# Hybrid encoder layer: operation costs of the order planner, spacing of the recurrent branch, and PSUM banks of its gates

## The chip, the cores and the metric

The kernel runs on one core of one Trainium2 chip. The metric is the device time of one execution in microseconds (us); less is better. Three executions of the kernel before took 1450.05, 1450.06 and 1452.24 us, median 1450.06. The profiled execution took 1451.69 us, and its trace spans 1449.9 us.

PE is TensorE (matmul; PEld is its weight load), DVE is VectorE, ACT is ScalarE, and SP issues all DMAs.

## The reference, cut to what matters

One layer over 1024 tokens of width 1024, float32, without batch:

```
h = rms_norm(x)
q, k, v, u, y, g_att, g_rec = split(h @ w_in + b_in)        # 512,512,512,1024,1024,1024,1024 columns
y_att = neighbourhood_attention(q, k, v, rpb) @ w_att_o     # 8 heads x 64
u = depthwise_conv4(u, conv_w, conv_b)
h_fwd, h_bwd = rg_lru(u, forward), rg_lru(u, backward)
   # r, i = sigmoid(block_diag(u) + b);  log_a = -8 r softplus(-lam);  a = exp(log_a)
   # h[t] = a[t] * h[t-1] + sqrt(1 - a[t]^2) * i[t] * u[t]
y_rec = ((h_fwd + h_bwd) * gelu(y)) @ w_rec_o
x = x + (sigmoid(g_att) * y_att + sigmoid(g_rec) * y_rec) @ w_out
x = x + square(relu(rms_norm(x) @ w_ff1)) @ w_ff2
return rms_norm(x)
```

## The kernel before, in words

**Number format and products.** Every float32 operand of a large product is split into a high part (an ACT copy with rounding: `wh`, `sh`, `uh`, `rh`) and a low part (a DVE subtraction: `wl`, `sl`, `ul`, `rl`); each product takes three matmuls (high x high, high x low, low x high). Nearly every matmul has a 128x128 weight tile and a 128x512 operand. The input projection and the feed-forward use a seven-product scheme for 2x2 block matrices: sums of weight blocks (`ws`, on DVE) and of activation blocks are formed once, and seven products replace eight.

**Stages, in order of time.** (1) RMSNorm of x, transposes on PE, the product for v, up to about 72 us. (2) The input projection of u, y, g (both gates) and q, k in 20 "pairs" (`pairs`, lines 627 to 654). A pair is seven products of 12 matmuls, 84 in all, on weights that ACT and DVE must have split before; the running sums of a pair (`r0`, `r1`) leave PSUM by an ACT copy or a DVE addition after each product (`ev1` to `ev7`). (3) Beside stage 2 run eight recurrent chains (lines 862 to 975), one per 128 channels of u: ACT adds the bias and takes the first tap of the convolution, DVE the other three (`uc`), a split gives `uh` and `ul`; four gates, each of six matmuls into two PSUM banks (`gate_pe`, lines 894 to 904), each bank evicted by an ACT sigmoid (`gate_act`); then tanh, exp, square, sqrt on ACT, multiplications and two scans on DVE (forward, backward), their sum, and the product with gelu(y). (4) Attention in 64 tiles between the matmuls of the recurrent output projection (`tprod`, lines 836 to 855, evicted by `evyr`, line 1151). (5) Attention output projection (evicted by `evya`, line 1177), output projection with the second norm, and feed-forward.

**What sets the order.** The program is not issued as it is written. A recorder (`Plan`, lines 109 to 332) notes each operation with its operands, a position and a cost in ns (lines 172 to 195). Positions count the steps of the PE main line, one step being six matmuls; `SD(position, ...)` places side work, lower positions first. `solve` (lines 204 to 324) runs a list schedule over these costs: an engine that is free takes the ready operation of lowest position, a pool tile is given when one is free. The operations are then issued in the order of their planned starts, so the costs and positions decide the order in every engine's queue, and nothing else of them reaches the chip. Because the recorder issues all, every instruction has line 332 in the profile.

**Pools.** SBUF tiles: 45 of `t`, 9 of `w`, 48 small ones. PSUM has eight banks of 128x512 float32. Pool `pm` has 2 slots of 128x1024 (two banks each), pool `pa` 4 slots of one bank. The pair products use both (`prod`, line 586); a 128x512 tile of `pm` takes a slot of two banks. Gates, transposes and attention take `pa`; `tprod` takes a whole `pm` slot of 128x1024.

**Placing of the chains.** `PORD` (line 825) is the order of the 20 pairs. A chain of u's pair starts at the end of that pair, the second chain of the pair `RSTEP` = 28 positions later; within a chain a step planned at t us sits t / `RRATE` positions behind the start, `RRATE` = 1.6. The attention tiles start `AOFF` = 3 positions after the products and stand `ASTEP` = 0.8 positions apart.

Tile names: `pa`, `pm` PSUM; `hTh`, `hTl` the transposed norm's two parts; `T1h` to `T4l` sums of these; `wh`, `wl`, `sh`, `sl`, `wx` weight blocks and their sums; `g` gate tiles, `th`, `sq` their temporaries; `r` running sums.

Of the kernel before, what the change touches and what calls it, by code (L numbers as in the profile page):

```python
# [106 lines left out]
class Plan:  # L107
# [11 lines left out]
    def add(self, eng, meth, args, kw):  # L119
# [9 lines left out]
        for v in rd + wr:  # L129
            if v.base.tag in ("pm", "pa"):  # L130
                for o in v.base.acc:
                    if o.eng != eng:
                        op.preds[o.idx] = 1
                v.base.acc.append(op)
# [37 lines left out]
        n = wr[0].free() if wr else 0  # L172
        psum = any(v.base.tag in ("pm", "pa") for v in rd)
        aps = sum(1 for k in ("scale", "bias") if isinstance(kw.get(k), VA))
# [3 lines left out]
        elif eng == "act":  # L178
            op.cost = n / 1.2 + (50 if psum else 94) + (93 if aps else 0) + (93 if "accum_out" in kw else 0)
            fn = args[2].name if hasattr(args[2], "name") else str(args[2]).split(".")[-1]  # L180
# [5 lines left out]
        elif eng == "dve":  # L186
            two = meth in ("tensor_copy", "tensor_scalar") and not psum
            aps = sum(1 for a in args[2:] if isinstance(a, VA) and a.free() == 1)
            op.cost = n / (1.92 if two else 0.96) + 68 + 60 * min(aps, 2) if n > 4 else 90
            if meth == "reciprocal":  # L190
                op.cost = 60 + 6.3 * n
        elif eng == "pool":
            op.cost = n * 2.2 + 60
        else:
            op.cost = 480
# [148 lines left out]
def emit(tc, x, prm, wst, wv, wg, watt, wrec, wout, wff1, wff2, tb, bv, lnf, out):  # L344
    nc = tc.nc
    from contextlib import ExitStack

    plan = Plan({"t": NSLOT - NW, "w": NW, "s": 48, "pm": 2, "pa": 4, "c": 64, "d": 128})
    pe, act, dve, pool, sp = [plan.engine(e) for e in ("pe", "act", "dve", "pool", "sp")]

    with ExitStack() as ctx:
# [18 lines left out]
        def PM():  # L370
            return VT(nm("pm"), (P, 1024), F32, "pm")

# [208 lines left out]
        def prod(o, a, ob, b, key, bank, first, ev, boost=5.0):  # L581

            for kk in range(2):
                def run(kk=kk):
                    if kk == 0 and first:
                        o.ps[key] = VT(nm("pm"), (P, 512), F32, "pm") if bank else PA()
                    hi, lo = o.lhs[a]()
# [168 lines left out]
        for t in range(8):  # L756

            def vq(t=t, o=Obj()):
                def run(q):
                    if q == 0:  # L760
                        o.ps = PM()
                    ps = o.ps[:, :512]
                    w = wvj[q]
# [44 lines left out]
        def st_qk(m):  # L808
            def store(r, half):
# [14 lines left out]

        PORD = (("u", 0), ("y", 0), ("g", 0), ("u", 1), ("y", 1), ("g", 1), ("g", 2), ("u", 2), ("y", 2), ("g", 3),
                ("g", 4), ("u", 3), ("y", 3), ("g", 5), ("g", 6), ("g", 7), ("qk", 0), ("qk", 1), ("qk", 2), ("qk", 3))
        FIRST = {"u": 8, "y": 16, "g": 24}
        STORE = {"u": st_u, "y": st_y, "g": st_g, "qk": st_qk}
        RSTEP, RRATE, AOFF, ASTEP = 28.0, 1.6, 3.0, 0.8
        B0 = here()  # L830
# [5 lines left out]
        def tprod(w, objs, kk=KD, wsel=None):  # L836

            o = Obj()
            for k in range(kk):
                def run(k=k):  # L840
                    if k == 0:
                        o.ps = PM()
                    wh = w.hi if wsel is None else w.hi[:, wsel]
                    wl = w.lo if wsel is None else w.lo[:, wsel]
                    for b in range(2):
                        c = slice(b * 512, (b + 1) * 512)
                        pe.matmul(o.ps[:, c], wh[:, k, :], objs.at("h", k, b * 512, 512), start=(k == 0), stop=False)
                    for b in range(2):
                        c = slice(b * 512, (b + 1) * 512)
                        pe.matmul(o.ps[:, c], wh[:, k, :], objs.at("l", k, b * 512, 512), start=False, stop=False)  # L850
                    for b in range(2):
                        c = slice(b * 512, (b + 1) * 512)
                        pe.matmul(o.ps[:, c], wl[:, k, :], objs.at("h", k, b * 512, 512), start=False, stop=(k == kk - 1))
                o.last = M(run)
            return o
# [6 lines left out]
        for j in range(8):  # L862
# [31 lines left out]
            def gate_pe(ty, d, R=R, j=j):  # L894
                w = wgj[j // 2]
                wh = w.hi[:, j % 2, ty * 2 + d, :]
                wl = w.lo[:, j % 2, ty * 2 + d, :]
                pss = R.g[ty, d] = [PA(), PA()]
                for b in range(2):
# [245 lines left out]
        for j in range(8):  # L1145
# [5 lines left out]
            def evyr(o=o, j=j):  # L1151
                dve.scalar_tensor_tensor(yr[j], yr[j], 1.0, o.ps, ALU.add, ALU.mult)
                yrd[j] = Dr("yrd")
                sp.dma_start(yrd[j], yr[j])
# [14 lines left out]
        for j in range(8):  # L1169
# [7 lines left out]
            def evya(o=o, j=j):  # L1177
                dve.scalar_tensor_tensor(ya[j], ya[j], 1.0, o.ps, ALU.add, ALU.mult)
                dve.tensor_add(ya[j], yr[j], ya[j])
                for b in range(2):  # L1180
                    split(mx.at("h", j, b * 512, 512), mx.at("l", j, b * 512, 512), ya[j][:, b * 512:(b + 1) * 512])
            SD(o.last + 0.1, evya, 30.0)
# [337 lines left out]
        for tag, n in plan.slots.items():  # L1520
            if tag == "c":
                pools[tag] = ctx.enter_context(tc.tile_pool(name="cp", bufs=1))
            elif tag == "d":
                pools[tag] = ctx.enter_context(tc.tile_pool(name="dp", bufs=1, space=bass.MemoryType.DRAM))
            elif tag in ("pm", "pa"):
                pools[tag] = ctx.enter_context(tc.tile_pool(name=tag, bufs=1, space=bass.MemoryType.PSUM))
# [81 lines left out]
```

## Time and profile before

| | before |
|---|---|
| median of three executions | 1450.06 us |
| profiled execution | 1451.69 us |
| span of its trace | 1449.9 us |
| granted TensorE clock, mean over the span | 0.995 |
| PE busy | 1413.8 us, 98% |
| DVE busy | 1043.6 us, 72% |
| ACT busy | 851.2 us, 59% |
| pair products with recurrent chains | 74.79 to 517.70 us, 442.91 us |

A busy share is the time in which an engine had an instruction under way. PE's matmuls overlap, so a busy PE may still start its matmuls further apart than it could; the distance of starts shows that. A wait in the profile is the idle time in front of an instruction, with the instruction that released it. A granted clock of 1.00 is TensorE at its full 2.4 GHz, and a slice's clock below 1.00 means that part of the slice ran at 1.2 GHz.

### The profile page before, as it was taken

How to read it: one execution, taken by the hardware profiler on the slowest of the kernel's cores; microseconds unless marked ns; L12 is line 12 of the kernel's file. 1: busy time of each engine (PE TensorE's matmuls, PEld its weight loads, DVE VectorE, ACT ScalarE, POOL GpSimd, SP SyncE). 2: the span in 40 equal slices, each digit the busy share in tenths (PEclk: the TensorE clock that was granted, in tenths of full speed). 3: DMA queues.
4: the chain of work that ended last, by engine and by line, in shares of the span. 5: the costliest groups of instructions: out<-in, count | busy, mean ns of one | idle time of the engine just before them, and what ended most of it. 6: DMA issues, size and time to landing. Idle time of an engine off the chain costs nothing.

```text
span 1449.9 us, 17675 instructions
## 1 busy us (share of the span) xinstructions
PE 1413.8 (98%) x6544; PEld 1150.9 (79%) x6544; DVE 1043.6 (72%) x1566; ACT 851.2 (59%) x1321; POOL 0.7 (0%) x6
## 2 busy tenths in 40 slices
PE   7999989999999999999999999999999999999997
PEld 5877767777877877787888878888888888888886
DVE  7996777778776477774764687665555867858995
ACT  7857877767864476764535555555555634332543
POOL 0000000000000000000000000000000000000000
PEclk9999999999999999999999999999999999999999
DMA  6514143143233494563923325444447893245402
GB/s 218 155 59 131 54 148 118 59 145 116 102 117 131 156 379 172 197 211 120 412 83 131 112 99 200 163 160 160 148 146 261 291 341 120 95 148 201 139 33 91
DMA packets 86935, 229.04 MB, mean 158 GB/s; under 512 B 8512, under 2 KB 16832, under 8 KB 86848
## 3 DMA queue, kind: packets, MB, share of 16 engines
q1 hardware_dynamic: 86848, 227.91, 45.2%
q8 instruction: 51, 0.84, 0.2%
q14 instruction: 36, 0.29, 0.1%
HBM read 158.67 MB, written 69.21 MB: 157 GB/s over the span
## 4 chain that ended last, share of the span: by engine, by line
PE 54%; DVE 4%; ACT 1%; issue 1%; DVEq 0%; ACTq 0%
PE pa L332 37%; PE pm L332 17%; DVE acc L332 1%; DVE wl L332 1%; DVE rl L332 1%; ACT fo L332 0%; DVE nu L332 0%; DVE h L332 0%; DVE x L332 0%; ACT h L332 0%; DVE F L332 0%; DVE fo L332 0%; DVE nr L332 0%; DVE T2l L332 0%; ACT wh L332 0%
## 5 line engine op out<-in xcount | busy, mean ns | idle before, releaser
L332 PE MATMUL pa<-wh,rh 128*128 128x512 f32 x448 | 174.1, 389 | 0.3 <-ACT rh L332 0.3
L332 PE MATMUL pa<-wl,rh 128*128 128x512 f32 x448 | 174.1, 389 | 0.0
L332 PE MATMUL pa<-wh,rl 128*128 128x512 f32 x448 | 174.0, 389 | 0.0
L332 ACT ACTIVATE r<-r 128x1024 f32<-128x1024 f32 x64 | 67.8, 1060 | 76.6 <-DVE r L332 75.2
L332 ACT ACTIVATE r<-pm 128x512 f32<-128x512 f32 x102 | 59.9, 588 | 73.9 <-PE pm L332 73.9
L332 DVE TENSOR_TENSOR wl<-ws,wh 128x1024 fp32r<-128x1024 f32 x64 | 77.7, 1220 | 33.9 <-ACT wh L332 33.3
L332 ACT ACTIVATE rh<-rs 128x1024 fp32r<-128x1024 f32 x56 | 58.7, 1049 | 70.8 <-PE pa L332 44.1
L332 ACT ACTIVATE sh<-ws 128x1024 fp32r<-128x1024 f32 x72 | 75.9, 1059 | 39.3 <-DVE ws L332 39.1
L332 PEld LDWEIGHTS pa<-wh,rh 128*128 128x128 f32 x448 | 84.0, 188 | 18.0 <-ACT rh L332 0.7
L332 PEld LDWEIGHTS pa<-wl,rh 128*128 128x128 f32 x448 | 84.0, 188 | 17.9 <-DVE wl L332 0.4
L332 PEld LDWEIGHTS pa<-wh,rl 128*128 128x128 f32 x448 | 84.1, 188 | 17.7 <-DVE rl L332 0.2
L332 ACT ACTIVATE wh<-w 128x1024 fp32r<-128x1024 f32 x56 | 58.8, 1051 | 56.7 <-PE pa L332 41.3
L332 PE MATMUL pm<-T4h,wx 128*128 128x512 f32 x272 | 90.0, 391 | 1.7 <-DVE r L332 1.6
L332 DVE TENSOR_TENSOR sl<-ws,sh 128x1024 fp32r<-128x1024 f32 x72 | 87.2, 1217 | 2.7 <-ACT sh L332 2.7
L332 DVE TENSOR_TENSOR r<-pa,r 128x512 f32<-128x512 f32 x74 | 50.7, 685 | 48.1 <-PE pa L332 48.0
L332 DVE TENSOR_TENSOR acc<-pa,acc 128x512 f32<-128x512 f32 x72 | 49.3, 686 | 47.9 <-PE pa L332 47.9
L332 DVE TENSOR_TENSOR wl<-w,wh 128x1024 fp32r<-128x1024 f32 x56 | 68.1, 1217 | 9.5 <-ACT wh L332 8.0
L332 DVE TENSOR_TENSOR rl<-rs,rh 128x1024 fp32r<-128x1024 f32 x56 | 68.2, 1217 | 4.5 <-ACT rh L332 3.0
L332 ACT ACTIVATE wh<-ws 128x1024 fp32r<-128x1024 f32 x61 | 63.7, 1053 | 12.3 <-DMA ws<-in_wff_dram 4.4
L332 PEld LDWEIGHTS pm<-T4h,wx 128*128 128x128 f32 x272 | 51.0, 188 | 13.6 <-DVE r L332 3.0
L332 PE MATMUL pa<-T1h,sl 128*128 128x512 f32 x144 | 56.6, 393 | 0.7 <-DVE sl L332 0.7
L332 PE MATMUL pa<-T1h,sh 128*128 128x512 f32 x144 | 56.7, 394 | 0.0
(229 smaller groups left out, 3665.1 us busy)
## 6 DMA issues: line engine op xcount, KB each, us to landing
rs<-rd SPq DMA_DIRECT2D x56, 512.0 KB, 7.5
ws<-in_wst_dram SPq DMA_DIRECT2D x41, 512.0 KB, 4.2
ws<-in_wff_dram SPq DMA_DIRECT2D x36, 512.0 KB, 4.4
w<-in_wff_dram SPq DMA_DIRECT2D x32, 512.0 KB, 7.8
B<-in_tb_dram SPq DMA_DIRECT2D x32, 384.0 KB, 5.2
x<-in_x_dram SPq DMA_DIRECT2D x16, 512.0 KB, 8.6
gd<-r SPq DMA_DIRECT2D x16, 512.0 KB, 3.0
g<-gd SPq DMA_DIRECT2D x16, 512.0 KB, 7.9
```

What stands on the lines that cost most here:

```text
L332: getattr(eng[op.eng], op.meth)(*[r(a) for a in op.args], **{k: r(a) for k, a in op.kw.items()})
```

## The change

Five edits, of which the first changes no instruction and sets only the planner's input:

1. The costs: an ACT operation of n elements is planned at 0.863 n + 168 ns (before: n / 1.2 + 94, or + 50 from PSUM), a DVE operation at 1.043 n + 151 ns (before: n / 0.96 + 68), a scan at 2.08 n + 151 ns (before: as any other DVE operation); small operations at 160 ns instead of 90.
2. PSUM: `pm` has 2 slots of one bank, a new pool `pr` 2 slots of one bank, `pa` its 4. The gates take `pr` instead of `pa`. `tprod` takes one tile of `pm` and one of `pr`.
3. `evyr` and `evya` work on two halves of 128x512 instead of one 128x1024.
4. `PORD` places u's second to fourth pairs one, one and two places later and y's second and third one earlier each.
5. `RSTEP` 28 to 33, `RRATE` 1.6 to 1.0, `AOFF` 3 to 1, `ASTEP` 0.8 to 0.75.

PE, ACT and SP execute as many instructions of the program as before (6354, 1227 and 534), DVE 24 more (1592 for 1568), all of edit 3.

```diff
         elif eng == "act":
-            op.cost = n / 1.2 + (50 if psum else 94) + (93 if aps else 0) + (93 if "accum_out" in kw else 0)
+            op.cost = n * 0.863 + 168 + (85 if aps else 0) + (190 if "accum_out" in kw else 0)
...
-            op.cost = n / (1.92 if two else 0.96) + 68 + 60 * min(aps, 2) if n > 4 else 90
+            op.cost = n * (0.522 if two else 1.043) + 151 + 60 * min(aps, 2) if n > 4 else 160 + 55 * min(aps, 2)
+            if meth == "tensor_tensor_scan":
+                op.cost = n * 2.08 + 151
+            if "accum_out" in kw:
+                op.cost += 85
             if meth == "reciprocal":
-                op.cost = 60 + 6.3 * n
+                op.cost = 152 + 6.3 * n
...
-    plan = Plan({"t": NSLOT - NW, "w": NW, "s": 48, "pm": 2, "pa": 4, "c": 64, "d": 128})
+    plan = Plan({"t": NSLOT - NW, "w": NW, "s": 48, "pm": 2, "pr": 2, "pa": 4, "c": 64, "d": 128})
...
         def PM():
-            return VT(nm("pm"), (P, 1024), F32, "pm")
+            return VT(nm("pm"), (P, 512), F32, "pm")
+
+        def PR():
+            return VT(nm("pr"), (P, 512), F32, "pr")
...
-        PORD = (("u", 0), ("y", 0), ("g", 0), ("u", 1), ("y", 1), ("g", 1), ("g", 2), ("u", 2), ("y", 2), ("g", 3),
-                ("g", 4), ("u", 3), ("y", 3), ("g", 5), ("g", 6), ("g", 7), ("qk", 0), ("qk", 1), ("qk", 2), ("qk", 3))
+        PORD = (("u", 0), ("y", 0), ("g", 0), ("y", 1), ("u", 1), ("g", 1), ("g", 2), ("y", 2), ("u", 2), ("g", 3),
+                ("g", 4), ("y", 3), ("g", 5), ("u", 3), ("g", 6), ("g", 7), ("qk", 0), ("qk", 1), ("qk", 2), ("qk", 3))
...
-        RSTEP, RRATE, AOFF, ASTEP = 28.0, 1.6, 3.0, 0.8
+        RSTEP, RRATE, AOFF, ASTEP = 33.0, 1.0, 1.0, 0.75
...
                     if k == 0:
-                        o.ps = PM()
+                        o.ps = [PM(), PR()]
...
-                pss = R.g[ty, d] = [PA(), PA()]
+                pss = R.g[ty, d] = [PR(), PR()]
...
             def evyr(o=o, j=j):
-                dve.scalar_tensor_tensor(yr[j], yr[j], 1.0, o.ps, ALU.add, ALU.mult)
+                for b in range(2):
+                    t = yr[j][:, b * 512:(b + 1) * 512]
+                    dve.scalar_tensor_tensor(t, t, 1.0, o.ps[b], ALU.add, ALU.mult)
...
             def evya(o=o, j=j):
-                dve.scalar_tensor_tensor(ya[j], ya[j], 1.0, o.ps, ALU.add, ALU.mult)
-                dve.tensor_add(ya[j], yr[j], ya[j])
                 for b in range(2):
-                    split(mx.at("h", j, b * 512, 512), mx.at("l", j, b * 512, 512), ya[j][:, b * 512:(b + 1) * 512])
+                    c = slice(b * 512, (b + 1) * 512)
+                    t = ya[j][:, c]
+                    dve.scalar_tensor_tensor(t, t, 1.0, o.ps[b], ALU.add, ALU.mult)
+                    dve.tensor_add(t, yr[j][:, c], t)
+                    split(mx.at("h", j, b * 512, 512), mx.at("l", j, b * 512, 512), t)
```

Three places show how it moves instructions. The first is on PE, the third gate of the second recurrent chain, before: six matmuls on `uh` and `ul`, written to tiles 1537 and 1539 of `pa`, between matmuls of the pair (on `T4` in `pm`).

```order
L332 MATMUL pm_1264<-T4l_890,wx_1332 128x512
L332 MATMUL pm_1264<-T4h_811,wx_1332 128x512 x2
L332 MATMUL pm_1264<-T4l_890,wx_1332 128x512
L332 MATMUL pm_1264<-T4h_811,wx_1332 128x512
L332 MATMUL pa_1537<-uh_1209,wh_1030 128x512
L332 MATMUL pa_1539<-uh_1209,wh_1030 128x512
L332 MATMUL pa_1537<-ul_1221,wh_1030 128x512
L332 MATMUL pa_1539<-ul_1221,wh_1030 128x512
L332 MATMUL pa_1537<-uh_1209,wl_1042 128x512
L332 MATMUL pa_1539<-uh_1209,wl_1042 128x512
```

After, the same gate writes tiles 1615 and 1620 of `pr`, and its neighbours are a `T1` product in `pa` and a `T3` product in `pm`.

```order
L336 MATMUL pa_1596<-T1l_997,sh_1498 128x512
L336 MATMUL pa_1596<-T1h_666,sl_1510 128x512
L336 MATMUL pr_1615<-uh_1298,wh_986 128x512
L336 MATMUL pr_1620<-uh_1298,wh_986 128x512
L336 MATMUL pr_1615<-ul_1533,wh_986 128x512
L336 MATMUL pr_1620<-ul_1533,wh_986 128x512
L336 MATMUL pr_1615<-uh_1298,wl_1040 128x512
L336 MATMUL pr_1620<-uh_1298,wl_1040 128x512
L336 MATMUL pm_1506<-T3h_627,sh_1498 128x512
L336 MATMUL pm_1506<-T3l_871,sh_1498 128x512
```

The gate no longer shares a pool with the products, and it stands at the boundary of two products instead of inside one. Over stage 2, the gates of the eight chains lie further apart: the last of them stood 443 matmuls before the stage's end, and stands 211 before it now.

The second place is on DVE, at the end of the second chain, before: the scans stand as SCALAR_TENSOR_TENSOR on three `g` tiles, and `wl_1800` is the low part of a weight block that PE waits for.

```order
L332 TENSOR_TENSOR g_1568<-g_1568,th_1606 128x1024
L332 SCALAR_TENSOR_TENSOR g_1522<-g_1481,g_1522 128x1024
L332 TENSOR_TENSOR sl_1774<-ws_1535,sh_1761 128x1024
L332 SCALAR_TENSOR_TENSOR g_1568<-g_1548,g_1568 128x1024
L332 TENSOR_TENSOR g_1780<-g_1780,uc_1556 128x1024
L332 TENSOR_TENSOR wl_1800<-ws_1754,wh_1789 128x1024
L332 TENSOR_TENSOR g_1522<-g_1522,g_1568 128x1024
L332 TENSOR_TENSOR sl_1813<-ws_1589,sh_1802 128x1024
L332 TENSOR_TENSOR g_1522<-g_1522,y_1731 128x1024
```

After, the same end of the second chain:

```order
L336 TENSOR_TENSOR sl_1840<-ws_1690,sh_1824 128x1024
L336 TENSOR_TENSOR g_1598<-g_1598,th_1679 128x1024
L336 SCALAR_TENSOR_TENSOR g_1598<-g_1560,g_1598 128x1024
L336 TENSOR_TENSOR g_1668<-g_1668,th_1687 128x1024
L336 TENSOR_TENSOR sl_1890<-ws_1715,sh_1878 128x1024
L336 SCALAR_TENSOR_TENSOR g_1668<-g_1633,g_1668 128x1024
L336 TENSOR_TENSOR wl_1915<-ws_1837,wh_1887 128x1024
L336 TENSOR_TENSOR r_318_1913<-pa_1880,r_318_1913 128x512
L336 TENSOR_TENSOR g_1895<-g_1895,uc_1734 128x1024
L336 TENSOR_TENSOR g_1598<-g_1598,g_1668 128x1024
```

The second scan still stands ahead of a weight's low part, but the two summed weights `sl` and the multiplications around it are dealt out differently, and the rest of the chain (the sum of both directions) comes two places later.

The third place is on ACT in the first stage, where `h` is the square sum of a tile of x, `ns` a root, `wh` a high part of v's weights and `hTh` the eviction of transposes that v's product reads, before:

```order
L332 ACTIVATE wh_210<-ws_100 128x1024
L332 ACTIVATE h_220,ss_221<-x_105 128x1024
L332 ACTIVATE ns_227<-ss_221,epst_79 128x1
L332 ACTIVATE h_238,ss_239<-x_118 128x1024
L332 ACTIVATE hTh_156<-pa_249,pr_88 128x128 x2
L332 ACTIVATE hTh_165<-pa_249,pr_88 128x128 x2
```

After:

```order
L336 ACTIVATE h_213,ss_214<-x_108 128x1024
L336 ACTIVATE ns_222<-ss_214,epst_82 128x1
L336 ACTIVATE h_227,ss_228<-x_121 128x1024
L336 ACTIVATE ns_236<-ss_228,epst_82 128x1
L336 ACTIVATE h_239,ss_240<-x_127 128x1024
L336 ACTIVATE ns_254<-ss_240,epst_82 128x1
L336 ACTIVATE h_258,ss_259<-x_195 128x1024
L336 ACTIVATE hTh_157<-pa_261,pr_91 128x128 x2
L336 ACTIVATE hTh_166<-pa_261,pr_91 128x128 x2
```

Two more square sums (of `x_127` and `x_195`) and two more roots stand ahead of the second group of `hTh`.

## Rows read from the trace of the kernel before

**Rows 1.** The page's busy times; share of the span, instructions.
```profile
PE 1413.8 (98%) x6544; PEld 1150.9 (79%) x6544; DVE 1043.6 (72%) x1566; ACT 851.2 (59%) x1321; POOL 0.7 (0%) x6
```

**Rows 2.** Windows: us; PE, PEld, DVE, ACT, POOL busy (instructions); clock, DMA share, GB/s.
```profile
74.79:517.70 442.91, 426.84 (x1826) 342.24 (x1824) 329.51 (x367) 308.29 (x367) 0.00 (x0) 0.99 0.34 118
181.25:217.50 36.25, 32.61 (x128) 25.12 (x127) 28.41 (x26) 28.79 (x33) 0.00 (x0) 0.91 0.42 148
290.00:326.25 36.25, 34.09 (x143) 27.49 (x142) 28.14 (x29) 22.91 (x31) 0.00 (x0) 0.95 0.41 145
498.00:540.00 42.00, 41.82 (x203) 33.69 (x202) 30.25 (x46) 32.90 (x47) 0.00 (x0) 1.00 1.04 370
906.25:942.50 36.25, 36.25 (x162) 30.01 (x161) 22.67 (x30) 19.88 (x24) 0.00 (x0) 1.00 0.49 163
```

**Rows 3.** Chain of waits, one piece: start, length, engine, tile, instructions.
```profile
1137.05 238.05 PE pa L332 x1049
```

**Rows 4.** PE's waits in stage 2: us in total, times, longest.
```profile
PE pa L332 <- DVE r L332: 2.9, 2, 2.2
PE pm L332 <- DVE wl L332: 2.6, 1, 2.6
PE pm L332 <- ACT r L332: 1.8, 3, 1.0
PE pa L332 <- ACT uh L332: 1.6, 2, 0.9
PE pm L332 <- DVE r L332: 1.6, 2, 1.4
PE pm L332 <- ACT wh L332: 1.5, 2, 1.1
PE pa L332 <- ACT g L332: 1.0, 1, 1.0
PE pa L332 <- DVE ul L332: 0.9, 2, 0.6
PE pm L332 <- DVE sl L332: 0.8, 1, 0.8
PE pa L332 <- DVE sl L332: 0.7, 1, 0.7
PE pm L332 <- ACT sh L332: 0.5, 1, 0.5
```

**Rows 5.** Timeline, a gate before: start, length, work, [idle in front <-releaser].
```profile
149.12 0.67 ACT L332 ACTIVATE g<-pa,pr 128x512 f32<-128x512 f32 x1
...
150.64 1.25 ACT L332 ACTIVATE g<-pa,pr 128x512 f32<-128x512 f32 x2
...
151.36 0.50 PE L332 MATMUL pa<-uh,wh 128*128 128x512 f32 x1 [0.98 <-ACT g L332]
```

**Rows 6.** Timeline, DVE and PE at the end of the second chain.
```profile
183.60 2.28 DVE L332 TENSOR_TENSOR_SCAN g<-g,g 128x1024 f32<-128x1024 f32 x1
...
185.81 1.20 DVE L332 TENSOR_TENSOR sl<-ws,sh 128x1024 fp32r<-128x1024 f32 x1
...
186.92 2.28 DVE L332 TENSOR_TENSOR_SCAN g<-g,g 128x1024 f32<-128x1024 f32 x1
...
189.12 1.20 DVE L332 TENSOR_TENSOR g<-g,uc 128x1024 f32<-128x1024 f32 x1
...
190.24 1.22 DVE L332 TENSOR_TENSOR wl<-ws,wh 128x1024 fp32r<-128x1024 f32 x1
...
191.51 0.79 PE L332 MATMUL pm<-hTh,wl 128*128 128x512 f32 x1 [2.63 <-DVE wl L332]
...
192.53 0.63 PE L332 MATMUL pa<-T1h,sh 128*128 128x512 f32 x1
...
192.96 0.63 PE L332 MATMUL pa<-T1l,sh 128*128 128x512 f32 x1
```

**Rows 7.** Timeline, ACT in the first stage.
```profile
19.74 1.14 ACT L332 ACTIVATE hTh<-pa,pr 128x128 fp32r<-128x128 f32 x4 [2.15 <-PE pa L332]
```

More of the change, by code (lines that the diff above doesn't have):

```diff
@@ L129, in add @@
         for v in rd + wr:
-            if v.base.tag in ("pm", "pa"):
+            if v.base.tag in ("pm", "pr", "pa"):
                 for o in v.base.acc:
@@ L172, in add @@
         n = wr[0].free() if wr else 0
-        psum = any(v.base.tag in ("pm", "pa") for v in rd)
+        psum = any(v.base.tag in ("pm", "pr", "pa") for v in rd)
         aps = sum(1 for k in ("scale", "bias") if isinstance(kw.get(k), VA))
@@ L585, in run @@
                     if kk == 0 and first:
-                        o.ps[key] = VT(nm("pm"), (P, 512), F32, "pm") if bank else PA()
+                        o.ps[key] = PM() if bank else PA()
                     hi, lo = o.lhs[a]()
@@ L761, in run @@
                         o.ps = PM()
-                    ps = o.ps[:, :512]
+                    ps = o.ps
                     w = wvj[q]
@@ L841, in run @@
                     if k == 0:
-                        o.ps = PM()
+                        o.ps = [PM(), PR()]
                     wh = w.hi if wsel is None else w.hi[:, wsel]
                     wl = w.lo if wsel is None else w.lo[:, wsel]
[L845 to L853, printed above, removed]
+                    for wt, part in ((wh, "h"), (wh, "l"), (wl, "h")):
+                        for b in range(2):
+                            pe.matmul(o.ps[b], wt[:, k, :], objs.at(part, k, b * 512, 512),
+                                      start=(k == 0 and wt is wh and part == "h"),
+                                      stop=(k == kk - 1 and wt is wl))
                 o.last = M(run)
@@ L1151, in evyr @@
             def evyr(o=o, j=j):
-                dve.scalar_tensor_tensor(yr[j], yr[j], 1.0, o.ps, ALU.add, ALU.mult)
+                for b in range(2):
+                    t = yr[j][:, b * 512:(b + 1) * 512]
+                    dve.scalar_tensor_tensor(t, t, 1.0, o.ps[b], ALU.add, ALU.mult)
                 yrd[j] = Dr("yrd")
@@ L1524, in emit @@
                 pools[tag] = ctx.enter_context(tc.tile_pool(name="dp", bufs=1, space=bass.MemoryType.DRAM))
-            elif tag in ("pm", "pa"):
+            elif tag in ("pm", "pr", "pa"):
                 pools[tag] = ctx.enter_context(tc.tile_pool(name=tag, bufs=1, space=bass.MemoryType.PSUM))
```

## The prediction

> **What bounds the kernel now.** I read the page's busy times first, then the table of windows, then the waits of PE, then the timeline where a wait is long. The page says that TensorE sets the time: PE is busy in 98% of the span, DVE in 72%, ACT in 59% [rows 1]. A faster DVE or ACT is therefore worth only what PE stands idle or runs slowly. How much that is follows from PE's own best rate in this trace. In one piece of the chain of waits 1049 matmuls take 238.05 us, 0.2269 us each [rows 3]. The window at 906 us agrees: 162 matmuls in 36.25 us, PE busy throughout, clock 1.00 [rows 2].
>
> The change aims at the stretch of the 20 pairs with the eight recurrent chains, 74.79 to 517.70 us, 442.91 us long [rows 2]. It holds 20 x 84 products less the 48 that ran before 74.79 us, and 8 x 4 gates of 6: 1632 + 192 = 1824 matmuls. At 0.2269 us they would take 413.9 us. The excess is 29.0 us, and it is the whole of what this stretch can give.
>
> The excess has three parts. (1) Idle: 442.91 - 426.84 = 16.1 us [rows 2], in the table of waits as 18 waits of 15.9 us [rows 4]. (2) A lowered clock: the slices at 181 us and at 290 us show 0.91 and 0.95 [rows 2]. There, behind waits on weights, matmuls start 0.43 us apart (192.53, 192.96) [rows 6] instead of 0.227, that is at 1.2 GHz; I count 18 of them in the stretch, 18 x 0.20 = 3.6 us. (3) The rest, 29.0 - 16.1 - 3.6 = 9.3 us: starts further apart at the foot of each wait (a matmul that starts late counts as busy until its modelled end), and bubbles too short to be a wait.
>
> The waits by what they are for [rows 4]: low and high parts of weight blocks (`wl`, `wh`, `sl`, `sh`) 2.6 + 1.5 + 0.8 + 0.7 + 0.5 = 6.1 us; the bank of a gate (`pa` on DVE's `r` and on ACT's `g`) 2.9 + 1.0 = 3.9; the running sums that keep a `pm` bank 1.8 + 1.6 = 3.4; the gates' own operands (`uh`, `ul`) 1.6 + 0.9 = 2.5.
>
> **The costs.** The planner before takes any DVE operation of 1024 elements for 1024 / 0.96 + 68 = 1135 ns. The timeline shows such operations 1.11 to 1.13 us apart (185.81 to 186.92, 189.12 to 190.24), so that is right, but the scans hold DVE for 2.20 us (183.60 to 185.81, 186.92 to 189.12) [rows 6]. 16 scans x 1.07 us = 17 us of DVE work in this stretch are unplanned. What comes of it stands at 183 to 192 us: `wl` is issued at 190.24, behind two scans, and PE waits 2.63 us for it, then runs at half clock [rows 6]. With 2.08 n + 151 = 2281 ns the planner knows of it. The other costs rise to the whole duration (1219 ns for 1024 elements, against 1.22 us shown), which overstates what an operation keeps its engine by some 8%. That makes the plan cautious; it puts no work on an engine.
>
> Here one rule speaks otherwise. The Trainium skill, page "VectorE: DVE Perf Modes", section "The DRAIN you can't avoid", says that the next DVE operation doesn't start until the pipe is empty. By that rule an operation would hold DVE for its whole 1.22 us, and the new costs would be exact. The trace disagrees here: the operation of 1.20 us at 189.12 is followed 1.12 us later by one that waits for nothing of it [rows 6]; the same section exempts what is not held. I go by the distance of starts. By the rule DVE's heaviest pair would come to 21.9 us instead of 20.2, at most 1 or 2 us more in all.
>
> **The spread of the chains.** I put the order of DVE's and ACT's instructions, cut at each pair's last running sum, beside the distances of starts. A pair gives PE 84 x 0.227 = 19.1 us, with its share of gates 21.3 us. Before, DVE has 24.6 us in one pair and 21.8 to 21.9 in four more, ACT 24.8 and 22.6 in two, while the last eight pairs ask DVE for only 8 to 16. In the windows this shows as DVE busy for 28.4 and ACT for 28.8 of 36.25 us at 181 us [rows 2], near full where a chain crosses the weights. After, DVE has at most 20.2 and ACT over 21.3 once (22.2). So weights and operands are late in at most one or two pairs: of 6.1 + 2.5 us of waits I leave 2.5. The chain's own length, 31.5 positions instead of 20, delays nothing that PE needs soon: the last gate still stands 211 matmuls, 48 us, ahead of the recurrent output projection.
>
> **The banks.** The products keep `pa` to themselves: gates no longer take banks there, which removes 3.9. A product's tile in `pm` was followed by its successor in as few as 11 matmuls, now in 24 at the least; 24 x 0.227 = 5.4 us is ample for an eviction of 0.6 to 0.7 us, and I leave 1 of 3.4. In exchange the gates have two banks where they had four. A gate can start only when the gate before it was evicted by its two sigmoids. By the order, 17 of 31 gates follow at 4 to 6 matmuls, 0.9 to 1.4 us, the others at 8 or more. A sigmoid takes 0.67 us, and PE starts some 0.05 us behind it [rows 5]: 0.72 us if ACT is free, so nothing; if ACT has just begun another operation of 1.1 us, up to 0.98 us of wait, as one gate shows [rows 5]. Bounds: 0 and 17 x 0.98 = 16.7 us. ACT is busy for 308.29 of 442.91 us, 70% [rows 2]; half a blocked operation in 70% of cases is 0.4 us, less the slack of 0.2 on average: 17 x 0.2 = 3.4, and with its tails I take 4.5.
>
> **Start, attention, end.** On ACT the norms of two more x tiles stand ahead of the second group of `hTh`. ACT had idled 2.15 us there for the transposes [rows 7], which covers nearly two square sums of 1.06 us; I take +0.8 (from -0.3 to +1.5). At the stage's end DMA is saturated, share 1.04 [rows 2]; the last of the recurrent loads now stands behind q, k and three gathers of v on SP's queue, with some 3 to 5 us in hand: 0, at worst +4. The 24 added half-width DVE operations lie where DVE has room (22.67 of 36.25 us in the feed-forward is typical [rows 2]): 0. Later stages keep their order: 0.
>
> **Sum.** Of 29.0 us stay: weights and operands 2.5, sums 1.0, gates 4.5, the short bubbles' irreducible part and remaining tails 0.8: 8.8 back, 20.2 gained. With the start, 20.2 - 0.8 = 19.4, and 0.6 for some attention bubbles that denser tiles fill: 20.0. The profiled execution took 1451.69 us, 1.6 above the median: 1451.69 - 20.0 = 1431.7, in the median's terms 1430.1. I say 1430.
>
> **Rivals.** (a) *The gates starve on two banks.* Each gate waits for the sigmoids of the one before. For it: 17 tight successions, an ACT that is 70% busy, and 0.98 us where this happened once [rows 5]. Against it: sigmoids are placed right behind their gates. Price: 31 x 0.98 = 31 us against 25 us that the rest of the excess gives: 1450 - 25 + 31 = 1456. It decides from 25 / 31 = 0.8 us a gate. In this connection the Trainium skill, page "TensorE: Matmul & The Clock Gate", section "A second HAM failure mode: psum-queue depth-cycling", tells of a kernel in which cycling PSUM banks made PE idle briefly and its clock swing. Here the clock fell behind waits of 2 to 3 us on weights [rows 2, 6], and no row shows that short gate waits lower it.
>
> (b) *The waits move.* Costs that overstate make other work late: a weight's part that was early is now issued after a chain's step. Then only banks and sums give, 3.9 + 3.4 us less the new gate waits: 0 to 7, around 1445. For it: the second scan still stands ahead of a `wl` on DVE. Against it: the loads per pair.
>
> (c) *Nothing is gained*, because gates lose what scans give: within 2.9 us of 1450, 0.2%, about what a measurement of this kernel can tell from no change.
>
> **How the numbers follow.** Forecast 0.64 (1421 to 1438; 1421 is 1450 - 29, all the excess); (b) with a gain over 0.2% 0.22 (1438 to 1447); (c) 0.07; (a) or a late recurrent load 0.07. Faster 0.64 + 0.22 = 0.86, same 0.07, slower 0.07. The range leaves out half of (b)'s upper end, (c) and (a): 1420 to 1445.
>
> **What would show it.** Stretch 2 should take about 423 us. PE's waits there on `wl`, `wh`, `uh`, `ul` should shrink from 8.6 to about 2.5 us, waits of `pa` or `pm` banks on `r` from 2.9 + 1.8 + 1.6 = 6.3 to 1, new waits of `pr` on ACT's `g` should come to 2 to 5 us, and no slice should show a clock under 0.98. The forecast is wrong if `pr` waits exceed 10 us, if weights still cost over 5, or if the start or the stage's end takes more than 4 us.

## The result, and the profile after

The changed kernel takes 1440.31 us in the median (four executions, 1439.58 to 1440.83), the kernel before 1450.05 us beside it: ratio 0.9933, interval 0.9916 to 0.995. The gain is 9.7 us, where 20 were forecast. The stage that the change aims at gave more than forecast (26.7 us for 20.2); attention, from which the forecast took 0.6 us of gain, lost 10.4.

The windows of the changed kernel: the whole product stage, the same two slices as in [rows 2], and the attention stage; columns as there.

```profile
78.29:494.51 416.22, 414.54 (x1825) 341.97 (x1824) 333.60 (x379) 308.32 (x366) 0.00 (x0) 1.00 0.36 125
181.25:217.50 36.25, 36.25 (x161) 30.03 (x160) 32.34 (x34) 32.56 (x38) 0.00 (x0) 1.00 0.31 102
290.00:326.25 36.25, 36.25 (x162) 30.01 (x161) 34.32 (x36) 24.20 (x29) 0.00 (x0) 1.00 0.30 103
494.51:679.24 184.73, 184.73 (x1090) 143.20 (x1089) 121.17 (x314) 117.64 (x240) 0.00 (x0) 1.00 0.59 200
```

The product stage takes 416.2 us for 442.9: of the 29.0 us of excess, 26.7 are gone, more than the 20.2 forecast. Both slices now hold 161 and 162 matmuls, as many as the slice at 906 us of [rows 2], where PE never idles. The clock is 1.00 in both. The waits of PE in that stage (columns as in [rows 4]) have shrunk from 15.9 us to 1.7; there is no row for `wl`, `wh`, `sl`, `uh` or `ul`, and none for `pr`:

```profile
PE pm L336 <- ACT r L336: 0.7, 1, 0.7
PE pa L336 <- ACT r L336: 0.7, 1, 0.7
PE pa L336 <- DVE T1l L336: 0.3, 1, 0.3
```

The attention stage of the kernel before, the row to hold against the last window above:

```profile
517.70:692.02 174.32, 173.88 (x1089) 137.58 (x1088) 122.49 (x306) 115.70 (x238) 0.00 (x0) 1.00 0.61 208
```

The same matmuls take 184.7 us instead of 174.3. PE counts as busy throughout in both, so neither a busy share nor the table of waits shows these 10.4 us. They show in the instructions that write or read `V`, 384 records for 192 matmuls (each is two records), first before, then after:

```profile
517.70:692.02 174.32, 34.92 (x384) 24.93 (x384) 1.00 0.61 208
```

```profile
494.51:679.24 184.73, 45.55 (x384) 31.55 (x384) 1.00 0.59 200
```

These are the products of the attention probabilities (`ab`) with v. One head has 64 columns, so its matmul fills half of PE's columns (`128*64` in the rows); the code issues three matmuls for one head and three for the other alternately. The timeline of PE in the kernel before shows a group of all six (x12) and the matmul behind it:

```profile
606.88 0.88 PE L332 MATMUL pa<-ab,V 128*64 128x128 f32 x12
607.69 0.73 PE L332 MATMUL pm<-rh,wh 128*128 128x512 f32 x2
```

Six matmuls take 0.81 us from start to the next start. In the changed kernel:

```profile
593.16 0.87 PE L336 MATMUL pa<-ab,V 128*64 128x128 f32 x6
593.96 0.51 PE L336 MATMUL pm<-rl,wh 128*128 128x512 f32 x1
594.39 0.87 PE L336 MATMUL pa<-ab,V 128*64 128x128 f32 x6
595.19 0.44 PE L336 MATMUL pa<-kh,qs 128*128 128x384 f32 x1
```

(`kh` and `qs` are the operands of the attention scores.) Here each head's three stand alone, and three take 0.80 us, as long as six alternated. Counted in the order of both kernels' instructions, 123 of these matmuls are followed at once by one of the other head before, 64 after; these are called alternations below. The groups, unbroken rows of such matmuls, rise from 41 to 58.

The stretches of all runs, from the starts of the first matmul of each stage in the traces (us; "start" is up to the first product of the pairs on one of the sums `T`, behind 48 others; "FF1" goes from the first matmul on `B11` to the first of the second feed-forward product, which is "FF2"). The stretches are those of one execution of each kernel, the median is that of all: the executions of the kernel before ran from 1447.4 to 1452.6 us, those with the lowest times at a granted clock of 0.999 and those with the highest at 0.995, so a few us of a difference between two stretches can be the execution's.

| | start | products | attention | to FF1 | FF1 | FF2 | median |
|---|---|---|---|---|---|---|---|
| before | 74.8 | 442.9 | 174.3 | 131.5 | 313.4 | 304.9 | 1450.1 |
| after | 78.3 | 416.2 | 184.7 | 130.6 | 317.1 | 304.0 | 1440.3 |
| av_pair | 77.8 | 416.2 | 166.4 | 130.6 | 317.1 | 304.0 | 1421.7 |
| pair_seq | 78.5 | 416.2 | 174.8 | 130.6 | 317.0 | 304.0 | 1430.1 |
| before_av_pair | 74.8 | 442.1 | 168.7 | 131.4 | 313.4 | 304.9 | 1445.2 |
| costs_only | 77.0 | 445.7 | 186.0 | 130.8 | 317.1 | 304.0 | 1471.0 |
| old_costs | 75.3 | 429.0 | 179.5 | 131.5 | 313.4 | 304.9 | 1443.4 |
| banks_only | 75.5 | 438.8 | 174.9 | 131.5 | 313.4 | 304.9 | 1448.8 |
| spread_only | 74.8 | 428.9 | 175.1 | 131.4 | 313.4 | 304.9 | 1438.6 |
| banks_back | 77.6 | 423.6 | 184.7 | 130.6 | 315.5 | 304.0 | 1446.7 |
| scan_true | 75.6 | 419.5 | 179.5 | 131.5 | 313.4 | 304.8 | 1434.1 |
| small_old | 77.2 | 417.7 | 184.7 | 130.6 | 316.2 | 304.0 | 1438.6 |
| mix_pair | 75.2 | 414.4 | 166.9 | 131.5 | 313.4 | 304.8 | 1416.1 |
| mix_pair_att | 74.6 | 414.4 | 168.5 | 131.5 | 313.4 | 304.9 | 1417.5 |
| same_half2 | 75.7 | 414.4 | 178.2 | 131.5 | 313.4 | 304.9 | 1428.0 |
| four_alt2 | 75.3 | 414.4 | 165.8 | 131.6 | 313.4 | 304.9 | 1415.0 |

### The profile page after: what moved, and what is told of

The parts are those of the page before. It is cut to its first block, busy times and chain, and to the rows that moved or that the text cites. A ratio compares the mean times of both kernels' runs of the same rounds, so it can differ in the third digit from the quotient of the medians.

```text
span 1439.0 us, 17698 instructions
## 1 busy us (share of the span) xinstructions
PE 1413.8 (98%) x6544; PEld 1159.2 (81%) x6544; DVE 1042.2 (72%) x1590; ACT 854.2 (59%) x1321; POOL 0.7 (0%) x6
## 4 chain that ended last, share of the span: by engine, by line
PE 97%; DMA 1%; DVE 1%; ACT 1%; issue 0%; SPq 0%
PE pa L336 56%; PE pm L336 33%; PE pr L336 8%; DMA x<-in_x_dram 1%; DMA ws<-in_wv_dram 0%; ACT h L336 0%; DVE T4l L336 0%; DVE T1l L336 0%; ACT hTh L336 0%; DVE h L336 0%; ACT r L336 0%; DVE sl L336 0%; ACT ns L336 0%; DVE nu L336 0%; ACT F L336 0%
## 5 line engine op out<-in xcount | busy, mean ns | idle before, releaser
L336 ACT ACTIVATE r<-r 128x1024 f32<-128x1024 f32 x64 | 67.7, 1060 | 68.2 <-DVE r L336 66.9
L336 ACT ACTIVATE sh<-ws 128x1024 fp32r<-128x1024 f32 x72 | 75.6, 1056 | 31.0 <-DVE ws L336 25.1
L336 DVE CUSTOM_DVE_ANT_0 ab<-pa,B 128x384 f32<-128x384 f32 x64 | 35.4, 556 | 39.6 <-PE pa L336 38.8
L336 ACT ACTIVATE ab<-pa 128x384 f32<-128x384 f32 x64 | 31.0, 484 | 45.6 <-PE pa L336 45.4
```

What stands on the lines that cost most here:

```text
L336: getattr(eng[op.eng], op.meth)(*[r(a) for a in op.args], **{k: r(a) for k, a in op.kw.items()})
```

## The experiments

**The two heads (av_pair, pair_seq, before_av_pair).** The edit gives the planner two more edges, so that the matmuls of both heads are planned when both are ready:

```diff
-            act.activation(o.pt, pt[:, :384], AF.Copy)
+            o.cp = act.activation(o.pt, pt[:, :384], AF.Copy)
...
-                    pe.matmul(ps[o.hd * DH:(o.hd + 1) * DH, o.n * P:(o.n + 1) * P],
+                    mm = pe.matmul(ps[o.hd * DH:(o.hd + 1) * DH, o.n * P:(o.n + 1) * P],
...
+                    mm.preds.setdefault(o0.cp.idx, 1)
+                    mm.preds.setdefault(o1.cp.idx, 1)
```

> The changed kernel with one edit: in attention, the product of the probabilities with v of two heads (12 records of 64 columns) is planned only when both heads are ready, so that their matmuls alternate. Theory (the loss in attention is lost alternation of the two heads): in the changed kernel a matmul followed by the other head's takes 0.122 us, by the same head's 0.233, at a group's end 0.301; alternations rise from 64 to 155 and groups fall from 58 to about 34, so 41.5 us of these matmuls become about 29, with their entries about 14 us less: attention stage 184.7 to about 171 us, time 1440.3 to about 1426. Rival (the stage is longer because its tiles stand denser and engines wait for one another): no change beyond 2 us, 1438 to 1442.

Measured 1421.73 us against 1440.31: 18.6 us less, attention 166.4. The theory holds, and the gain is larger than its 14 us. It had 12.5 from the matmuls themselves and some 1.5 from the entries, the matmuls in front of the groups. By the distances of starts in both traces the matmuls gave 14.4 (41.5 to 27.1) and the entries 5.8 (15.5 to 9.7); other places took some 2 back.

In pair_seq the two loops over heads and blocks are exchanged besides:

```diff
-            for b in range(3):
-                g = b + o0.hf
-                for o in (o0, o1):
+            for o in (o0, o1):
+                for b in range(3):
+                    g = b + o0.hf
```

> As av_pair, but the three matmuls of one head are issued before the three of the other: as few groups as in av_pair, nearly no alternation (29). Theory: alternation itself is what pays: 29 x 0.122 + 129 x 0.23 + 34 x 0.28 = 42.7 us against 41.5 in the changed kernel, some 2 us back at the entries: about 1439.5, attention stage about 184. Rival (what costs is the switch between 128-column and 64-column matmuls, so only the number of groups counts): as fast as av_pair, attention stage 171 to 175 us.

Measured 1430.13 us, attention 174.8: between the two. The theory's 184 us is missed by 9; of the rival, the 171 to 175 us of attention came true, but not that it is as fast as av_pair. Its groups of six:

```profile
580.96 1.14 PE L336 MATMUL pa<-ab,V 128*64 128x128 f32 x12
582.04 0.50 PE L336 MATMUL pm<-rl,wh 128*128 128x512 f32 x1
```

A group takes 1.08 us instead of 0.81, but less than twice the 0.80 of a lone head. By single records, the second head's first matmuls start beside the last ones of the first head: the overlap doesn't need strict alternation, it needs both heads in PE's queue near each other. So of the 18.3 us that av_pair takes from the stage, 9.9 come from having both heads in one group (with it the groups fall from 58 to 35) and 8.4 from alternating them.

> The kernel before with the same one edit as av_pair: alternations rise from 123 to 159. Theory: 36 x 0.11 us, with fewer groups about 4 us less in the attention stage (174.3 to about 170), time 1450 to about 1446. Rival (the stage's length comes from its density): no change.

Measured 1445.15 us against 1451.77 for before beside it (ratio 0.9957, 0.9943 to 0.997), attention 168.7: the same loss was in the kernel before, smaller. The theory's 4 us came out as 5.6 in the stage.

**Why it pays (same_half2, four_alt2).** Both are mix_pair (below) with groups of four tiles, and two banks for the two query groups. The order inside a group of 12 matmuls differs (same_half2 first, four_alt2 with the second line instead):

```diff
+                    for o in (o0, o2) if h == 0 else (o1, o3):   # same head, other query group and bank
...
+                    for o in (o0, o1) if h == 0 else (o2, o3):   # other head, other columns
```

> mix_pair with the matmuls of four attention tiles (two heads, two query groups) planned when all four are ready, 12 matmuls a group, the two query groups in PSUM banks of their own. Order: matmuls of one head alternate between the two query groups, so always the same 64 columns of PE and always another PSUM bank; then the other head. Theory (the two column halves of PE work beside each other): 0.17 to 0.23 us a matmul inside a group, as where heads don't alternate, 192 x about 0.18 = 34 us, time 1421 to 1426. Rival (a matmul that accumulates where the one before it did must wait for it; any other target will do): 0.12 us a matmul, time 1415.

> The same groups of four tiles and the same two banks, but the two heads alternate, as in mix_pair. Theory: 0.12 us a matmul inside a group; 17 to 20 groups instead of 34 take another 2 us from entries and exits unless the longer wait for four tiles makes gaps: time 1414 to 1417. If grouping is worth nothing: 1416 to 1418.

A group of 12 matmuls (x24) and what follows, in same_half2 and then in four_alt2:

```profile
605.82 2.46 PE L345 MATMUL pa<-ab,V 128*64 128x128 f32 x24
608.20 0.45 PE L345 MATMUL pa<-kh,qs 128*128 128x384 f32 x1
```

```profile
600.50 1.53 PE L345 MATMUL pa<-ab,V 128*64 128x128 f32 x24
601.97 0.45 PE L345 MATMUL pa<-kh,qs 128*128 128x384 f32 x1
```

2.38 us against 1.47. Alternating the place of accumulation gains nothing; alternating the column halves does. 1427.99 and 1415.02 us: the theory holds, the rival falls. same_half2 came out 2 us above its range, four_alt2 inside, 1.0 us below mix_pair. The two column halves also write to different halves of PSUM's partitions, and these runs don't tell which of the two lets them overlap.

**The costs (costs_only, old_costs, scan_true, small_old).** costs_only is the kernel before with edit 1 alone, old_costs the changed kernel without it.

> The kernel before with the new costs alone (edit 1): old banks, old order of pairs, old spacing. Theory: the costs bring most of what the product stage gained (of 26.7 us some 15), and they are also what breaks the alternation in attention (62 alternations in its order, as in the changed kernel's 64): stage of products about 428 us, attention about 185, time about 1448. Rival: the banks and the spacing bring the gain, the costs only the loss: products 440 us or more, time 1460.

Measured 1470.98 us, 19 us slower than before (ratio 1.014, 1.0124 to 1.0156). Attention loses as expected (186.0 us); the rest of the theory falls: products 445.7 us, none of the gain. PE's largest waits in the stage are again for gate operands, running sums and weights:

```profile
PE pa L336 <- ACT uh L336: 4.3, 3, 1.9
PE pm L336 <- ACT r L336: 3.8, 6, 0.7
PE pm L336 <- ACT wh L336: 3.3, 4, 1.3
```

The rival (products 440 us or more) is right, though its 1460 us is 11 short: start, attention and FF1 lose 2.2, 11.7 and 3.7 us here.

> The changed kernel with the costs of before (edit 1 undone), banks and spacing new. Theory (banks and spacing bring the gain in the product stage, the costs bring only the losses at the start, in attention and at the second norm): products 418 to 424 us against 416.2 in the changed kernel and 442.9 before, start 75 us as before, attention with 90 alternations in its order about 180 us against 184.7: time about 1433. Rival (the products need the scans' true cost too): products 430 us or more, time 1443 or more.

Measured 1443.39 us, products 429.0. Losses at the start and at FF1 are gone, as the theory has it, but its 418 to 424 us of products are missed, and the rival's 430 only by 1: of the 26.7 us gained, 14.0 come without the costs and 12.7 need them. In attention either edit breaks the alternation alone: the costs with the old placing (costs_only, 62 alternations, 186.0 us), and the new placing with the old costs (old_costs, 90, 179.5). Where both are old it stays at 122 to 124 (banks_only 174.9, spread_only 175.1 us). What PE waits for in the products of old_costs:

```profile
PE pm L332 <- DVE r L332: 5.7, 5, 1.6
PE pr L332 <- DVE ul L332: 1.1, 2, 0.9
PE pr L332 <- ACT g L332: 0.7, 1, 0.7
PE pr L332 <- ACT uh L332: 0.2, 1, 0.2
```

The running sums wait on DVE. Four of the five waits stand at the end of a stretch of DVE without a pause of 0.15 us or more that holds one or two scans; the fifth, of 1.3 us, has no scan in its stretch. scan_true adds to old_costs one line:

```diff
+            if meth == "tensor_tensor_scan":
+                op.cost = n * 2.08 + 151
```

> old_costs (banks and spacing new) with one cost of the new ones: the scan's, 2281 ns instead of 1135. Theory of the prediction (the 17 us of scans that the planner did not know of are what made weights and operands late): products fall from 429.0 to 420 us or less, time from 1443.4 to about 1434. Rival (it is the caution in all other costs, whole durations plus hand-over, that keeps waits away): products 426 to 430 us, time 1441 or more.

Measured 1434.06 us, products 419.5, and the 5.7 us are gone; all that is left in the stage's table:

```profile
PE pr L334 <- ACT g L334: 0.7, 1, 0.7
PE pr L334 <- ACT uh L334: 0.2, 1, 0.2
```

The theory holds. The scan's cost, put in first, is 9.4 us of the 12.7 that the costs give here; all other costs together are 3.3.

> The changed kernel with the cost of one-column DVE operations at 90 ns again (now 160). Theory (the chain of one-column operations between a norm's square sum and its scaling, planned too long, is put behind other work and makes PE's transposes late): products begin at about 75.5 us instead of 78.3, the stretch from B11's to the second feed-forward product 313.5 instead of 317.1, attention unchanged at 184.7: time about 1434. Rival (the costs of the large operations reorder these places): start and that stretch as in the changed kernel, time 1440.

Its edit is `else 90` for `else 160 + 55 * min(aps, 2)`. Measured 1438.57 us, start 77.2, FF1 316.2. The interval (0.99 to 0.9928, against 0.9916 to 0.995) doesn't separate it from the changed kernel; the waits do. The first line is the changed kernel's wait for the scaled tile `h` of the first norm's last tile, the second the changed kernel's wait in FF1, the third the same wait here:

```profile
55.55 1.09 PE L336 MATMUL pa<-ident,h 128*128 128x128 f32 x8 [1.26 <-DVE h L336]
825.13 1.96 PE L336 MATMUL pa<-ident,h 128*128 128x128 f32 x8 [3.37 <-DVE h L336]
824.60 1.09 PE L336 MATMUL pa<-ident,h 128*128 128x128 f32 x8 [2.52 <-DVE h L336]
```

All five runs with the new costs throughout (after, av_pair, pair_seq, costs_only, banks_back) have the first wait, 1.26 us each; here it is gone. So the theory holds for this wait and for a part of FF1's (1.0 us in the kernel before); the rest of FF1's comes from the other costs. With all old costs there (old_costs, mix_pair) FF1 takes 313.4 us as before.

**Banks and spacing (banks_only, spread_only, banks_back).** banks_only is the kernel before with edits 2 and 3; spread_only has the new `PORD` and `33.0, 1.0, 3.0, 0.8`; banks_back is the changed kernel with

```diff
-                pss = R.g[ty, d] = [PR(), PR()]
+                pss = R.g[ty, d] = [PA(), PA()]
```

> The kernel before with the new PSUM pools and the halved evictions alone (edits 2 and 3), costs and spacing old. Theory: only waits for banks go, 3.9 us of gates and about 2 of running sums, so products about 437 us and time about 1444. Rival (pa and pm banks were what upset the whole stage): products 425 us or less, time 1433. Second rival (two banks starve the gates of a chain that runs at the old pace): products above 443 us, slower than before.

> The kernel before with the new order of pairs and the spread chains alone (edit 4 and the first two numbers of edit 5). Theory: the even load takes most of the 8.6 us of waits for weights and gate operands with their clock and restart losses, products about 428 us, time about 1436. Rival (the chains lie closer in time of gates and products, so the shared banks go on costing): products 437 us or more, time 1445.

> The changed kernel with the gates back in the pool of the products (pa, four banks); pr is used by the recurrent projection alone. Theory: gates and products wait for each other's banks again, 4 us of waits and as much of restarts: products 422 to 426 us, time about 1447. Rival (with spread chains the pool does not matter): products within 2 us of 416, time about 1440.

banks_only: products 438.8, 4.1 us less; near its theory's 437, but its time is 1448.84 us, not 1444, near no change (ratio 0.999, 0.9981 to 0.9999). The waits for banks fall, as the theory has it, from 7.3 us (`r` 6.3, `g` 1.0) to 2.9, but those for `sl` rise from 1.5 us to 7.1. This is rival (b) of the prediction, waits that move:

```profile
PE pm L332 <- DVE sl L332: 5.0, 5, 1.6
PE pa L332 <- DVE sl L332: 2.1, 3, 0.8
```

spread_only: products 428.9, time 1438.63, near its theory (428, 1436): the largest single part, and alone as fast as all five edits together (ratio 0.992, 0.9907 to 0.9934, against 0.9916 to 0.995). banks_back: products 423.6, 1446.69, as its theory, though of its 5.9 us of waits 3.2 are for banks (`r`, `g`) and 2.4 for `sh` and `sl`. The second rival of banks_only (two banks starve the gates) falls.

**Costs where they help (mix_pair, mix_pair_att).** mix_pair is av_pair with

```diff
+            if self.lo <= self.pos < self.hi:     # lo, hi: first pair, recurrent projection
...
+            else:                                 # the costs of before
```

> av_pair with the new costs for work of the product stage alone (positions from the first pair to the recurrent projection); before and behind it the planner gets the costs of before. Theory (the new costs gain in the product stage and lose at the start, in attention and at the second norm): start 75.2 us, products 416 to 419, attention about 166.5 with 158 alternations, the stretch from B11's to the second feed-forward product 313.4 instead of 317.1: time about 1417 against 1421.7 for av_pair. Rival (the product stage's gain hangs on the order that the start leaves): products 425 us or more, time 1426.

Measured 1416.06 us (ratio to before 0.9758, 0.9745 to 0.9771), 24.3 us less than the changed kernel. Its two stages:

```profile
75.17:489.59 414.42, 413.96 (x1826) 342.12 (x1824) 329.94 (x368) 307.97 (x366) 0.00 (x0) 1.00 0.36 125
489.59:656.47 166.88, 166.87 (x1090) 132.82 (x1088) 120.78 (x314) 117.45 (x241) 0.00 (x0) 1.00 0.65 225
```

The products are 0.5 us from the 413.9 of PE's own rate, below the 416 to 419 expected. The theory holds.

> mix_pair with the attention tiles placed as before (AOFF 3.0, ASTEP 0.8). Theory (with alternation held, the placing of the tiles matters little): attention 166 to 169 us, time within 3 us of mix_pair. Rival (denser tiles cost by themselves, as old_costs with 179.5 against spread_only with 175.1 us seems to say): 4 us less than mix_pair.

Measured 1417.48 us, attention 168.5: placing matters by 1.6 us once the heads are kept together. The rival falls: the 4.4 us between old_costs and spread_only came with lost alternation (90 against 124).

## Why the prediction missed, step by step

**Attention, 0.6 us gained: this step failed.** It measured 10.4 us lost. The prediction read "denser tiles" from the positions and looked for engines that wait; it took an idle-free PE for one whose time is fixed by its matmuls, and said of costs that overstate an operation that they only make the plan cautious. The runs show that the new costs reorder other stages too: alone they make the kernel 19 us slower (costs_only), 11.7 of it in attention, where the two heads' matmuls alternate 62 times instead of 123. Neither the scan's cost nor that of the small operations does it (attention is the same in scan_true as in old_costs, and in small_old as in the changed kernel), so it comes from the rest of the costs. The order of the instructions is fixed before a run, so a count of the alternations (123 against 64) would have shown this without one. With the alternation repaired (av_pair) the kernel takes 1421.7 us, below the forecast 1430.

That 1440.3 us lies within the range given, 1420 to 1445, is luck: the products gained 6.5 us more than forecast, and attention, start and later stages lost 10.4, 3.5 and 1.9. By its time the result falls where the prediction put rival (b), 1438 to 1447, but in the product stage the waits shrank instead of moving. (The stretches sum to 10.9 us, the medians differ by 9.7: the profiled execution of the kernel before was 1.6 us above its median.) Of the signs that were to show the forecast wrong none came true, and none of them looked at attention.

**Products, 20.2 us gained.** Measured 26.7. The parts: spacing alone 14.0, banks alone 4.1, costs alone -2.8; together 26.7. The sum of single effects is 15.3, so 11.4 lie in their interplay. Under the old costs the banks add nothing to the spacing (spread_only 428.9, old_costs 429.0); under the new costs they bring 7.4 us (banks_back 423.6, changed kernel 416.2). The costs bring 5.3 us with the spacing alone (spread_only to banks_back, whose `pm` also has the new slots) and 12.7 with both. The scan's missing time is real (9.4 us between old_costs and scan_true), but costs_only has the same knowledge and no gain. That it takes the spacing, which leaves DVE room to put the scan elsewhere, fits these runs; a run with costs and banks without the spacing was not made, so this is argued.

**Gates on two banks, 4.5 us kept.** Measured 0: no wait of `pr` has a row. The estimate took ACT's busy share as the chance of a blocked sigmoid; that the planner, which knows the sigmoids' time, put the gates where ACT was free, would explain it, but is not shown. The count was off too: in the changed order 17 of 62 banks, in 10 of the 31 gates, are taken again after 4 to 6 matmuls, not 17 of 31 gates. With old costs the same banks cost 0.7 us of `g` with the new spacing (old_costs) and 1.9 with the old (banks_only). Rival (a) is out.

**Weights and operands 2.5, sums 1.0 kept.** Measured 0 and 1.4. Rival (b), that waits only move, fails in the changed kernel; banks_only shows it.

**Start, +0.8 us.** Measured +3.5, outside the bounds given. Two parts can be told apart. From PE's first transposes to the first product on a sum, the five runs with the new costs take 67.6 to 67.7 us and the ten with the old costs there 65.4 to 66.5; the changed kernel takes 2.2 us more than the kernel before. Of these, 1.26 us are the wait for the last `h` (small_old above, which takes 66.3 us without it); the other 0.9 were not taken apart. The place that the prediction named, `hTh` behind the norms, has a wait of 0.25 us. The rest of the 3.5 us, 1.3, is that the first transposes start at 10.65 instead of 9.32 us. DVE before, the first norm's chain and the first weight's high part:

```profile
6.19 0.27 DVE L332 TENSOR_SCALAR nu<-nr,na 128x1 f32<-128x1 f32 x1
6.50 0.15 DVE L332 TENSOR_SCALAR nu<-nu 128x1 f32<-128x1 f32 x1
6.57 0.68 DVE L332 CAST wh<-ws 128x1024 fp32r<-128x1024 f32 x1
```

After:

```profile
7.45 0.69 DVE L336 CAST wh<-ws 128x1024 fp32r<-128x1024 f32 x1 [1.36 <-DMA ws<-in_wv_dram]
8.06 0.27 DVE L336 TENSOR_SCALAR nu<-nr,na 128x1 f32<-128x1 f32 x1
...
9.38 0.15 DVE L336 TENSOR_SCALAR nu<-nu 128x1 f32<-128x1 f32 x1
```

The copy stands ahead of the norm's chain and waits 1.36 us for its DMA. But costs_only has the same order, gets its DMA earlier, and starts the first transposes at 9.25 us; the five runs with this order differ by up to 1.6 us here. So the new order makes the start depend on this DMA, and whether the 1.3 us belong to the order or to the execution stays open.

**Later stages, 0.** Measured +1.9: FF1 +3.7, the others -0.9 each. In the second norm the root `ns` now stands on ACT behind an eviction that waits for PE, and DVE's chain behind it:

```profile
821.80 0.60 ACT L336 ACTIVATE r<-pm 128x512 f32<-128x512 f32 x1 [0.47 <-PE pm L336]
822.29 0.28 ACT L336 ACTIVATE ns<-ss,epst 128x1 f32<-128x1 f32 x1
...
822.61 0.16 DVE L336 RECIPROCAL nr<-ns 128x1 f32<-128x1 f32 x1 [0.40 <-ACT ns L336]
```

PE's transposes of that tile start 3.76 us after the matmul in front of them instead of 1.41. Behind this wait the granted clock fell: matmuls start 0.43 us apart for a while instead of 0.23, that is at 1.2 GHz. The window behind the wait, in the changed kernel and in banks_back:

```profile
825.00:832.00 7.00, 6.87 (x27) 5.90 (x28) 4.83 (x13) 4.71 (x16) 0.00 (x0) 0.76 0.01 2
832.00:839.00 7.00, 7.00 (x36) 5.90 (x36) 6.13 (x13) 5.77 (x17) 0.00 (x0) 1.00 0.01 2
```

banks_back has the same wait of 3.37 us and kept its clock; its FF1 takes 315.5 us instead of 317.1. So 2.1 of the 3.7 us are the wait's and 1.6 the clock's; the clock fell in four of the five profiled executions with this wait (after, av_pair, pair_seq, costs_only). The prediction's "keep their order" rests on no row, and the order of the second norm had changed.

**The recurrent load at the stage's end, 0.** No wait for it in the changed kernel. Right.

## What to carry to other kernels

Costs of a list scheduler are a knob on every stage at once: compare the orders stage by stage, also where nothing was meant to change, and give a stage costs of its own if they serve only that one. An engine at 100% busy can still gain: compare the distance of starts of the same instructions before and after, since matmuls that could run side by side leave no wait when they don't. Of changes that act on one bottleneck, measure the parts both alone and as removals: here one part alone was slower and still carried 12.7 us of the whole.

## What the runs showed of the hardware

Matmuls of 64 columns on different column halves of PE run beside each other when they are close in the queue. Records on one half start 109 ns apart; alternated, a matmul of two records costs 0.114 us (four_alt2), in groups that change the half once 0.188 us (same_half2, means over the groups), and between two on the same half mostly 0.218 us (lone heads of the changed kernel). The Trainium skill, page "TensorEngine Tiling (Array Packing)", section "Key Properties", says that different tiles can load weights and multiply in parallel; the traces agree (1.47 against 2.38 us for the same 12 matmuls), and add that this holds only if the program's order brings the halves together. The same section says that changing the tiling mode drains TensorE; in the changed kernel a 128x512 matmul ahead of such a group is followed 0.34 us later by the group, against 0.24 us by another matmul, which agrees with a cost at the switch of some 0.1 us; no run isolates it.

DVE's scan holds the engine for 2.20 us at 128x1024, twice the 1.11 to 1.12 us of a TENSOR_TENSOR of that size [rows 6].
